# Layer 0's first convolution block: all late taps but the last as VectorE products with GpSimd sums, with moved far taps, another bank layout in layer 1 and a moved weight load

## The chip, the cores and the metric

One NeuronCore of a Trainium2 chip runs the whole kernel in one launch. The metric is the device time of one execution in microseconds (us). The engines are TensorE (PE in the profile, with its weight loads as PEld), VectorE (DVE), ScalarE (ACT), GpSimd (POOL) and SyncE (SP), which issues most of the loads and stores.

## The reference

Two encoder layers on 1024 tokens of width 1024, all in float32. Cut to what matters here:

```python
for l in range(DEPTH):
    h = _rmsnorm(x, g_mix[l])
    p = h @ w_in[l]
    q = (_rmsnorm(p[..., :o1], g_q[l]) @ w_uq[l])        # 8 heads, 64 + 32 rotary
    kv = (_rmsnorm(p[..., o1:o2], g_kv[l]) @ w_ukv[l])   # keys 64 and values 64 a head
    y_attn = _mla_attention(q_nope, q_rope, k_nope, k_rope, v)
    a, gt = jnp.split(p[..., o3:], 2, axis=-1)
    u = a * jax.nn.sigmoid(gt)                           # 512 channels
    u = _dwconv(u, w_dw_conv[l], b_dw_conv[l])           # 31 taps along the tokens
    u = jax.nn.silu(_layernorm(u, g_conv_ln[l], b_conv_ln[l]))
    x = x + jnp.concatenate([y_attn, u], axis=-1) @ w_o[l]
    z = _dwconv(_rmsnorm(x, g_ffn[l]) @ w_up[l], w_dw_ffn[l], b_dw_ffn[l])
    zg, zv = jnp.split(z, 2, axis=-1)
    x = x + (jax.nn.silu(zg) * zv) @ w_down[l]
return _rmsnorm(x, g_final)
```

The 31-tap depthwise convolution is what the change is about. Channels lie on the 128 partitions, so the 512 channels are four blocks (0 to 3) of 128 x 1024, and each tap is a shifted multiply and add of a whole block.

## The kernel before, in words

Every float32 matrix product is made of three products of split operands (an upper part `h` and a lower part `l`), with 512 columns a matmul. Each layer runs through three stages, each with its own set of the eight PSUM banks: `project` (all products with `w_in`, `w_uq` and `w_k`), `attention` (64 steps, one for each head and block of 128 queries), and `feed` (the output product `w_o`, then `w_up` and `w_down` with a sum scheme of seven products in place of eight). The order of instructions on each engine is the order in which the code is written; nothing reorders it.

The taps of the depthwise convolution are done in three ways, by the numbers of `NEAR_TAPS`, block for block:

- **Near taps** run in `project` on VectorE, one multiply-add each (`conv_step`). A small planner (`work`) writes them between the evictions of the projection, by a count of VectorE's time in `clock["dve"]`.
- **Far taps** run in `project` too (`tap_far`): ScalarE multiplies into a buffer of the tag `wr`, which has three, and GpSimd issues a DMA that adds the buffer to the block.
- **Late taps** are what is left, and run in `attention` (`tap_late`). By default GpSimd multiplies and issues a DMA that adds the product to the block (`kinds` "pool"). For the first taps of block 0 listed in `STEP_AT` for layer 0, VectorE makes the product at a given step and GpSimd adds it to the block with an instruction of its own one step later (kind "step"). In layer 1 all late taps go the first way.

All adds to one block depend on each other: a sum of GpSimd on block 0 waits until the last accumulating DMA on block 0 has landed, and a DMA that adds to a block waits for the one before it on the same block. GpSimd runs its list in order. On the same list stand `yt<-yt,rb` (the division of a pair of heads, line 1670), whose result ScalarE splits eight steps after the even head's turn (`ys_3h`, line 194), and from step 50 the four loads of `wo` (line 915), whose lower parts ScalarE begins at step 55 (line 175). ScalarE runs in order too; it also copies half of every transposed probability tile (`pt`, line 1610), and VectorE the other half (line 1611). TensorE needs both for the next transposes (`t`) and for the value product (`o`).

In `attention` PSUM holds two wide tiles of two banks (scores `s`, later also the spread reciprocals `rc_70s` and the early output sums `po_e`), two single banks (`pv`, `o`, later `rc_71s`) and two banks `t0`, `t1` for transposes. A stage hands out banks in the order in which its tags are first used, so `pv` of the first two row tiles, which use `t0` and `t1`, get the first two banks of the set. At the end of a head `gather` adds the two halves of `o`: a copy on ScalarE (line 1647) and an add on VectorE (line 1648). For the last head `divide` (line 1683) and `finish` (the split `ys_7h`, `ys_7l`) follow. `next_sections` begins layer 1: norms, then the first three products, with `supply` calling for the loads and the lower parts of later weights.

Of the kernel before, what the change touches and what calls it, by code (L numbers as in the profile page):

```python
# [9 lines left out]
F32 = mybir.dt.float32  # L10
# [56 lines left out]
MANUAL = [E.PE, E.DVE, E.Activation, E.Pool]  # L67
LATE_COST = {"pool": 2.3, "step": 0.0}
LATE_STEPS = 0
STEP_AT = ((8, 12, 16, 20, 30, 36, 46, 50), ())  # L70
LATE_FROM = 2
NEAR_TAPS = ((8, 16, 18, 16), (16, 17, 18, 16))
BEGIN = (-5.7, -20.2)
GLU_AT = (-1.7, -14.9)
KEY_AT = (4.0, -8.6)
# [44 lines left out]
class Encoder:  # L120
# [395 lines left out]
    def next_sections(self, l, nxt, supply):  # L516
        names = ("g0", "a0", "g1")
        w = [self.complete(*e) for e in nxt["w"]]
        for k in range(8):
            self.norm_apply(l, nxt["x"], nxt, 1, k)  # L520
        self.norm_sums(l, nxt["x"], nxt, 1, range(4, 8))
        supply(-16.0)
        self.pp.tile([128, T], F32, name=f"skip{l}", tag="w1", bufs=1)
        ps = [self.wide(f"p{n}{l}") for n in names]
        self.key_weight(l, nxt["wk"])
        self.upper_first(ps[0], self.tiled(w[0]), nxt["hl"], HALVES[0])
        for i, c in ((1, 0), (0, 1), (1, 1)):
            for k in range(8):
                self.partial(ps[i], self.tiled(w[i]), nxt["hl"], k, (c,))
                if (i, c, k) == (0, 1, 3):  # L530
                    self.norm_spread(l, nxt, 1, self.bank)
            if (i, c) == (1, 0):
                self.norm_root(l, nxt, 1, self.bank)
        keys = self.key_products(l, nxt["wk"], lambda k, c: nxt["x"][k][:, c])
        for c in range(2):
            for k in range(8):
                self.partial(ps[2], self.tiled(w[2]), nxt["hl"], k, (c,))
        return nxt["hl"], nxt["r"], dict(zip(names, ps)), lambda: keys
# [38 lines left out]
    def project(self, l, carry):  # L577
        nc, a = self.nc, self.a
        par = self.par[l]
        clock = {"pe": 0.0, "dve": 0.0}  # L580
# [29 lines left out]
        def launch(steps, n=-1):  # L610
            active.append([clock["pe"], steps, n])

        def finish(n):
            for e in [e for e in active if e[2] <= n]:
                for step in e[1]:
                    clock["dve"] = max(clock["dve"], e[0]) + step[0]
                    e[0] = clock["dve"] + step[1]
                active.remove(e)
# [13 lines left out]
        def glu(j):  # L632
# [6 lines left out]
            todo = [t for t in range(KC) if t != PAD]  # L639
            taps.extend((j, t) for t in todo[:NEAR_TAPS[l][j]])  # L640
            taps.sort(key=lambda e: NEAR_ORDER.index(e[0]))
            away[j] = todo[NEAR_TAPS[l][j]:]
            far_at[j] = 0.0
# [210 lines left out]
        times, starts, t = {}, {}, 0.0  # L854
# [6 lines left out]
        def supply(now, turn=TURN):  # L861
            while coming and coming[0][1] <= now + LEAD:
                name, at = coming.pop(0)
                turning.append((name, at, self.cast(l, name)))
            while turning and turning[0][1] <= now + turn:
                name, at, e = turning.pop(0)
                w[name] = self.complete(*e)
# [10 lines left out]
        for n, (name, weight, emit, evict, after) in enumerate(seq):  # L878
            supply(clock["pe"])
            finish(n - 3)  # L880
            ps[name] = self.wide(f"p{name}{l}")
            emit()
            clock["pe"] += times[name]
            queue = [i for i, _ in taps]
            far = [j for j in away if clock["pe"] >= far_at[j] and
                   (j not in queue or queue.count(j) == NEAR_TAPS[l][j] and queue.index(j) > 8)]
            for j in sorted(far, key=far_at.get)[:FAR_TOGETHER if times[name] > 5.0 else 0]:
                self.tap_far(l, j, away[j].pop(0), u[j], conv[j])
                far_at[j] = clock["pe"] + FAR_GAP
            work(clock["pe"])  # L890
            if after:
                after()
            launch(evict(), n)
# [27 lines left out]
    def feed(self, l, conv, ys, ready, casts, x):  # L921
        nc, a, par = self.nc, self.a, self.par[l]
        left, right = HALVES
        steps, at = [], defaultdict(list)

        def put(step, rank, f):
            at[step].append((rank, len(at[step]), f))

        self.wo_steps(l, conv, ys, ready, casts, x, steps, put)
        self.up_steps(l, steps, put)  # L930
        out = self.down_steps(l, steps, put)
        for n in range(min(at), len(steps)):
            if n >= 0:
                steps[n]()
            for _, _, f in sorted(at.pop(n, ()), key=lambda e: e[:2]):
                f()
        return out
# [619 lines left out]
    def attention(self, l, u, conv, away, spill, keys, kvs, loaded, ahead, wo, begun):  # L1557
# [2 lines left out]

        qd, qrd, kd = spill
        state, v = {}, []

        def rows(tt):
            (kv, wv), ts = kvs, slice(tt * 128, (tt + 1) * 128)
# [50 lines left out]
        def values(pair, n):  # L1616
            h, qp = divmod(pair, 4)
            st = state[h]
            e = h % 2
            gg = qp // 2  # L1620
            main, aux = slice(e * 64, e * 64 + 64), slice(64 - e * 64, 128 - e * 64)
            if qp % 2 == 0:
                if gg == 0 and e == 0:
                    st["y"], st["rb"] = self.blk(f"yt{l}_{h}"), self.blk(f"rb{l}_{h}")
                elif gg == 0:
                    st["y"], st["rb"] = state[h - 1]["y"], state[h - 1]["rb"]
                st["po"] = self.bank(f"o{l}_{h}_{gg}")
            po = st["po"]
            cs = slice(qp % 2 * 256, qp % 2 * 256 + 256)
            for g in range(2):  # L1630
                pt = st["pt"].pop((qp, g)).rearrange("p k q r t -> p k (q r t)")
                for i in range(4):
                    k = 4 * g + i
                    nc.tensor.matmul(po[ROW_TILES[i % 2], cs], v[k // 2][:, k % 2, h * 64:h * 64 + 64], pt[:, i, :],  # L1634
                                     start=k < 2, stop=k > 5)
            if qp % 2 == 0:
                return
            if n >= total:
                gather(h, gg, main, aux, n)
            else:  # L1640
                agenda[n].append(lambda: gather(h, gg, main, aux, n))

        def gather(h, gg, main, aux, n):
            st = state[h]
            y, rb, po = st["y"], st["rb"], st["po"]
            qs = HALVES[gg]
            nc.scalar.copy(out=y[main, qs], in_=po[aux, :])
            nc.vector.tensor_tensor(out=y[main, qs], in0=po[main, :], in1=y[main, qs], op=ALU.add)
            if h < HEADS - 2:
                if gg:  # L1650
                    agenda[n + 1].append(lambda: turned(h, main, rb, y))
            elif n > total:
                divide(y[main, qs], main, h, gg)
            else:
                agenda[n + 1].append(lambda: divide(y[main, qs], main, h, gg))
                if h == last:
                    agenda[n + 1].append(lambda: finish(last, y, 0))
# [24 lines left out]
        def divide(ym, main, h, c):  # L1682
            nc.vector.tensor_tensor(out=ym, in0=inv.pop((h, c))[main, :], in1=ym, op=ALU.mult)
# [10 lines left out]
        def finish(h, y, c):  # L1694
            cs = HALVES[c]
            if c == 0:
                ys.append([self.blk(f"ys{l}_{h}{i}", F32R) for i in "hl"])
            hi, lo = (t[:, cs] for t in ys[-1])
            nc.scalar.copy(out=hi, in_=y[:, cs])
            nc.vector.scalar_tensor_tensor(out=lo, in0=y[:, cs], scalar=1.0, in1=hi.bitcast(F32), op0=ALU.mult, op1=ALU.subtract)  # L1700
# [3 lines left out]
        agenda = defaultdict(list)  # L1704
        late = sorted(((i + 0.5) / len(away[j]), j, t) for j in range(4) for i, t in enumerate(away[j]))
        stepped = [i for i, (_, j, _) in enumerate(late) if j == LATE_STEPS][:len(STEP_AT[l])]
        kinds = ["step" if i in stepped else "pool" for i in range(len(late))]
        costs = [LATE_COST[kind] for kind in kinds]
        for i, (_, j, t) in enumerate(late):
            n = LATE_FROM + int((SIDE_TIME - LATE_FROM) * sum(costs[:i]) / sum(costs))  # L1710
            if kinds[i] == "step":
                m, tap = STEP_AT[l][stepped.index(i)], self.tap_late(l, j, t, u[j], conv[j], nc.vector)
                agenda[m].insert(0, lambda tap=tap: next(tap))
# [7 lines left out]
        last = HEADS - 1  # L1721
# [11 lines left out]
        for n in range(-2, total + 1):  # L1733
            if n % 2 and n > 2:
                values((n - 3) // 2, n)
# [8 lines left out]
            if n + 2 < total:  # L1744
                h, qt = divmod(n + 2, 8)
# [199 lines left out]
```

## Time and profile before

| what | value |
|---|---|
| median of 3 runs | 2239.71 us (2237.3 to 2240.65) |
| profiled execution, its own time | 2242.22 us |
| its span, first to last instruction | 2240.5 us |
| TensorE busy | 2221.1 us, 99% of the span, 12750 matmuls |
| VectorE busy | 1666.4 us, 74% |
| ScalarE busy | 1240.2 us, 55% |
| GpSimd busy | 681.7 us, 30% |
| mean granted TensorE clock | 0.997 |
| chain that ended last | 86% TensorE, 5% VectorE, 3% issue, 3% DMA |

Busy time is summed over the whole span. A share says nothing of a single stage. "Granted clock" is the part of TensorE's full 2.4 GHz that the chip gave it; 0.5 is its lower level of 1.2 GHz.

### The profile page before, as it was taken

What the parts mean: (1) busy time and instruction counts of PE and PEld (TensorE: products, weight loads), DVE (VectorE), ACT (ScalarE), POOL (GpSimd) and SP (SyncE); (2) the same over time, 40 slices, a digit from 0 to 9 for tenths busy, and PEclk for the clock granted to TensorE, in tenths of its full rate; (3) what the DMA queues carried; (4) which work ended last, traced back from release to release, by engine and by line L of the source; (5) the groups of instructions that cost most, each with busy time, mean ns of one, the idle gap of its engine ahead of it and who ended that gap; (6) DMA issues with size and microseconds to landing.
All of it is one profiled execution on the core that took longest, in us unless ns stands there. A gap on an engine that the chain in (4) does not pass through costs nothing.

```text
span 2240.5 us, 34453 instructions
## 1 busy us (share of the span) xinstructions
PE 2221.1 (99%) x12750; PEld 1780.0 (79%) x12750; DVE 1666.4 (74%) x2213; ACT 1240.2 (55%) x1896; POOL 681.7 (30%) x791
## 2 busy tenths in 40 slices
PE   9999999999999999999999999999999999999998
PEld 7887666788888888888878876668888888888887
DVE  7998777668877776776579877776787777768765
ACT  5454776446655555544533557774575555555444
POOL 1232666332333333001412224652323333320032
PEclk9999999999999999999999999999999999999999
DMA  5799997765899998935957999976578999988366
GB/s 184 169 201 280 215 188 172 204 173 122 219 278 305 273 296 207 338 101 138 214 145 156 214 268 209 212 182 180 149 173 221 299 291 284 289 209 298 96 130 167
DMA packets 197928, 473.29 MB, mean 211 GB/s; under 512 B 24224, under 2 KB 32128, under 8 KB 197760
## 3 DMA queue, kind: packets, MB, share of 16 engines
q0 software_dynamic: 98912, 221.08, 48.6%
q1 hardware_dynamic: 98272, 248.96, 33.5%
q8 instruction: 100, 1.64, 0.3%
q10 hardware_dynamic: 576, 1.05, 0.1%
q14 instruction: 68, 0.56, 0.1%
HBM read 305.35 MB, written 80.40 MB: 172 GB/s over the span
## 4 chain that ended last, share of the span: by engine, by line
PE 86%; DVE 5%; issue 3%; DMA 3%; POOL 1%; ACT 1%; SPq 0%; POOLq 0%; ACTq 0%; DVEq 0%
PE p L1141 34%; PE pd L1329 17%; PE po L952 7%; PE s L1585 5%; PE o L1634 4%; PE pa L212 3%; PE t L1608 3%; PE pg L212 2%; PE pg L574 2%; PE pq L212 1%; PE pn L212 1%; DVE conv L1784 1%; PE pkv L212 1%; PE pa L574 1%; DVE mx L1587 1%
## 5 line engine op out<-in xcount | busy, mean ns | idle before, releaser
L1141 PE MATMUL p<-b,w 128*128 128x512 f32 x3552 | 807.2, 389 | 0.4 <-ACT zv L1152 0.3
L1141 PEld LDWEIGHTS p<-b,w 128*128 128x128 f32 x3552 | 666.0, 188 | 141.0 <-DVE w L1523 1.2
L1329 PE MATMUL pd<-ab,wd 128*128 128x512 f32 (+1 forms) x1920 | 422.3, 381 | 0.0
L1329 PEld LDWEIGHTS pd<-ab,wd 128*128 128x128 f32 x1920 | 350.7, 188 | 69.5 <-DVE ab L1523 0.4
L176 POOL DMA_DIRECT2D w<-wu x96 | 84.4, 880 | 358.2 <-ACT w L175 318.0
L1587 DVE TENSOR_REDUCE mx<-s 128x1 f32<-128x1024 f32 x128 | 156.3, 1221 | 38.3 <-PE s L1585 32.9
L1595 ACT ACTIVATE p<-s,mx 128x1024 f32<-128x1024 f32 x128 | 142.9, 1117 | 58.7 <-DVE mx L1587 56.2
L1535 DVE SCALAR_TENSOR_TENSOR o<-zg,par,o 128x1023 f32<-128x1023 f32 x88 | 112.8, 1283 | 76.5 <-ACT o L1529 75.1
L1784 DVE SCALAR_TENSOR_TENSOR conv<-gate,par,conv 128x1023 f32<-128x1023 f32 (+14 forms) x125 | 159.1, 1275 | 4.5 <-ACT conv L636 1.5
L176 POOL DMA_DIRECT2D w<-in_w_up x116 | 100.6, 868 | 202.0 <-ACT w L175 178.5
L1611 DVE COPY pt<-t 128x512 f32<-128x512 f32 x128 | 87.9, 687 | 64.1 <-PE t L1608 62.3
L175 ACT ACTIVATE w<-w 128x512 fp32r<-128x512 f32 x212 | 133.6, 630 | 3.0
L1634 PE MATMUL o<-pt,v 128*64 128x256 f32 x1024 | 129.3, 390 | 5.2 <-DVE pt L1611 2.3
L1090 DVE TENSOR_TENSOR zg<-p,zg 128x512 f32<-128x512 f32 x88 | 60.6, 690 | 99.1 <-PE p L1141 92.3
L1521 ACT CAST ab<-ac 128x512 fp32r<-128x512 f32 x130 | 80.1, 617 | 94.7 <-DVE ac L1264 93.3
L915 POOL DMA_DIRECT2D wd<-in_w_down x44 | 33.0, 750 | 308.1 <-PE pd L1329 301.1
L1535 DVE SCALAR_TENSOR_TENSOR v<-zv,par,v 128x1023 f32<-128x1023 f32 x88 | 112.5, 1280 | 10.4 <-ACT v L1529 10.3
L1521 ACT CAST w<-wu 128x512 fp32r<-128x512 f32 x84 | 51.9, 620 | 122.6 <-DVE wu L1090 122.6
L1634 PEld LDWEIGHTS o<-pt,v 128*64 128x64 f32 x1024 | 68.2, 137 | 57.5 <-issue 20.2
L1108 ACT CAST w<-wu 128x512 fp32r<-128x512 f32 x96 | 59.0, 614 | 93.0 <-DVE wu L1090 89.4
L1608 PEld LDWEIGHTS t<-ident,p 64*128 64x128 f32 x2048 | 77.1, 139 | 40.0 <-issue 27.4
L1523 DVE TENSOR_TENSOR ab<-ac,ab 128x512 fp32r<-128x512 f32 x130 | 89.3, 689 | 24.8 <-ACT ab L1521 17.7
(2123 smaller groups left out, 4304.3 us busy)
## 6 DMA issues: line engine op xcount, KB each, us to landing
w<-in_w_up POOLq DMA_DIRECT2D x232, 256.0 KB, 7.5
wu<-in_w_up SPq DMA_DIRECT2D x88, 512.0 KB, 4.8
w<-wu POOLq DMA_DIRECT2D x96, 256.0 KB, 5.6
sd<-in_w_down SPq DMA_DIRECT2D x44, 512.0 KB, 9.2
ws<-sd SPq DMA_DIRECT2D x44, 512.0 KB, 7.5
wd<-in_w_down POOLq DMA_DIRECT2D x88, 256.0 KB, 5.5
act<-v SPq DMA_DIRECT2D x36, 512.0 KB, 6.1
ac<-act SPq DMA_DIRECT2D x72, 256.0 KB, 5.7
```

The costliest lines, as they stand in the source:

```text
L175: self.nc.scalar.activation(out=lo, in_=hi.bitcast(F32), func=AF.Copy, scale=-1.0)
L176: self.nc.gpsimd.dma_start(out=lo, in_=src, accum_op=ALU.add)
L212: nc.tensor.matmul(ps[:, HALVES[c]], w, x[:, HALVES[c]], start=(k == 0 and s == 0), stop=(k == n - 1 and s == 2))
L952: self.nc.tensor.matmul(ps, p[:, sl], q[:, cs], start=(k == 0 and t == 0), stop=(k == 3 and t == 2))
L1141: nc.tensor.matmul(ps, w[p][:, k * 128:(k + 1) * 128], b[:, q], start=(i in (1, 5, 2) and k == 0 and t == 0), stop=(k == 3 and t == 2), sk ...
L1329: nc.tensor.matmul(ps[t, m][:, cs], w[i, j][p][:, m * 128:(m + 1) * 128], b[:, q, cs], start=(i in (1, 5, 2) and j == 0 and s == 0), stop= ...
L1535: self.nc.vector.scalar_tensor_tensor(out=o[:, a:b], in0=z[:, at + a:at + b], scalar=self.par[l][:, tap:tap + 1], in1=o[:, a:b], op0=ALU.m ...
L1587: nc.vector.tensor_reduce(out=mx, in_=ps, op=ALU.max, axis=AX.X, negate=True)
L1595: nc.scalar.activation(out=p, in_=ps, func=AF.Exp, bias=mx, accum_out=st["sums"][:, qt:qt + 1])
L1608: nc.tensor.transpose(t[:, i, qi, :], st["p"][2 * qp + qi][r, ks], self.ident[r, r])
L1634: nc.tensor.matmul(po[ROW_TILES[i % 2], cs], v[k // 2][:, k % 2, h * 64:h * 64 + 64], pt[:, i, :], start=k < 2, stop=k > 5)
L1784: self.nc.vector.scalar_tensor_tensor(out=y[:, lo:hi], in0=u[:, lo + s:hi + s], scalar=self.tap(l, j, t), in1=y[:, lo:hi], op0=ALU.mult, o ...
```

## The change

Five edits:

1. Block 0 of layer 0 has 14 late taps. Before, 8 were VectorE products with GpSimd sums and 6 were GpSimd products with adding DMAs, mixed on one block. Now 13 are VectorE products with sums, at the steps listed, and the last tap alone is a GpSimd product with a DMA. Block 3 of layer 0 loses one near tap, which becomes a far one, and one that was far is now late; layer 1 gets three more near taps (two for block 0, one for block 2), and so three fewer late ones.
2. In `project`, VectorE work due in the first half of a section, and what ScalarE does with it, is written ahead of the far taps of that section.
3. In layer 1, `attention` uses its two wide tiles and its two single banks once before anything else, which gives them the first six banks, and `t0` and `t1` the last two; `feed` gets a matching order of its banks.
4. For the first half of the last head, `gather` is written one step later, in both layers, and what follows it too.
5. In `next_sections` the call `supply(-16.0)` stands behind the spread of the norm.

```diff
-STEP_AT = ((8, 12, 16, 20, 30, 36, 46, 50), ())
+STEP_AT = ((8, 10, 12, 14, 16, 18, 20, 30, 32, 34, 36, 46, 48), ())
-NEAR_TAPS = ((8, 16, 18, 16), (16, 17, 18, 16))
+NEAR_TAPS = ((8, 16, 18, 15), (18, 17, 19, 16))
...
-        supply(-16.0)
         self.pp.tile([128, T], F32, name=f"skip{l}", tag="w1", bufs=1)
...
                 if (i, c, k) == (0, 1, 3):
                     self.norm_spread(l, nxt, 1, self.bank)
+                    supply(-16.0)
...
+            work(clock["pe"] - times[name] / 2)
             for j in sorted(far, key=far_at.get)[:FAR_TOGETHER if times[name] > 5.0 else 0]:
                 self.tap_far(l, j, away[j].pop(0), u[j], conv[j])
...
         steps, at = [], defaultdict(list)
+        for i in (3, 2, 4, 5, 6, 7) if l else ():
+            self.pp.tile([128, 512], F32, name=f"lay{l}_{i}", tag=f"d{i}", bufs=1)
...
         state, v = {}, []
+        for i, f in enumerate((self.wide, self.wide, self.bank, self.bank) if l else ()):
+            f(f"lay{i}")
...
             if n >= total:
                 gather(h, gg, main, aux, n)
             else:
-                agenda[n].append(lambda: gather(h, gg, main, aux, n))
+                m = n + (h == last)
+                agenda[m].append(lambda: gather(h, gg, main, aux, m))
```

The first place is GpSimd's list in layer 0's attention, around the division of the second pair of heads (`late_0_27` is tap 27 of block 0, `conv_0` the block, `yt_2` the pair of heads). Before:

```order
L1796 TENSOR_SCALAR late_3_27_3357<-gate_3_821,par_63 128x1012
L1802 DMA conv_3_892<-late_3_27_3357 128x1012
L1796 TENSOR_SCALAR late_0_27_3399<-gate_0_417,par_63 128x1012
L1802 DMA conv_0_425<-late_0_27_3399 128x1012
L1800 TENSOR_TENSOR conv_0_425<-conv_0_425,late_0_22_3397 128x1017
L1796 TENSOR_SCALAR late_2_28_3504<-gate_2_665,par_63 128x1011
L1802 DMA conv_2_754<-late_2_28_3504 128x1011
L1670 TENSOR_TENSOR yt_2_2553<-yt_2_2553,rb_2_2554 128x1024
```

And now:

```order
L1802 TENSOR_SCALAR late_1_28_3404<-gate_1_420,par_63 128x1011
L1808 DMA conv_1_570<-late_1_28_3404 128x1011
L1806 TENSOR_TENSOR conv_0_425<-conv_0_425,late_0_27_3402 128x1012
L1802 TENSOR_SCALAR late_2_28_3509<-gate_2_662,par_63 128x1011
L1808 DMA conv_2_751<-late_2_28_3509 128x1011
L1676 TENSOR_TENSOR yt_2_2557<-yt_2_2557,rb_2_2558 128x1024
L1802 TENSOR_SCALAR late_3_27_3558<-gate_3_818,par_63 128x1012
L1808 DMA conv_3_886<-late_3_27_3558 128x1012
L1802 TENSOR_SCALAR late_3_28_3643<-gate_3_818,par_63 128x1011
L1808 DMA conv_3_886<-late_3_28_3643 128x1011
```

The sum ahead of `yt_2` no longer stands behind an adding DMA on the same block; taps 27 and 28 of block 3 now follow each other.

The second place is ScalarE in layer 0's projection, where the keys' and queries' latents are split (`far_0_16` is a far tap's product, `kvs`, `cqs` the split latents that TensorE needs next). Before:

```order
L175 ACTIVATE wu20l<-wu20h 128x768
L1790 ACTIVATE far_0_16_1221<-gate_0_417,par_63 128x1023
L1790 ACTIVATE far_1_21_1224<-gate_1_420,par_63 128x1018
L1790 ACTIVATE far_2_20_1227<-gate_2_665,par_63 128x1019
L664 ACTIVATE qss_1_1233<-cq_1231 128x1024
L720 ACTIVATE kvs_0h<-ckv_965,par_63 128x1024
L720 ACTIVATE kvs_1h<-ckv_1037,par_63 128x1024
L720 ACTIVATE cqs_1h<-cq_1231,par_63 128x1024
```

And now:

```order
L175 ACTIVATE wu20l<-wu20h 128x768
L664 ACTIVATE qss_1_1224<-cq_1222 128x1024
L720 ACTIVATE kvs_0h<-ckv_956,par_63 128x1024
L720 ACTIVATE kvs_1h<-ckv_1030,par_63 128x1024
L720 ACTIVATE cqs_1h<-cq_1222,par_63 128x1024
L1796 ACTIVATE far_0_16_1240<-gate_0_417,par_63 128x1023
L1796 ACTIVATE far_1_21_1243<-gate_1_420,par_63 128x1018
L1796 ACTIVATE far_2_20_1246<-gate_2_662,par_63 128x1019
```

The three far products moved behind the four splits.

The third place is VectorE at the end of layer 0's attention (the same rows stand in layer 1). Before:

```order
L1587 TENSOR_REDUCE mx_7_7_4573<-s_7_7_4562 128x1
L1648 TENSOR_TENSOR yt_6_4073<-o_7_0_4434,yt_6_4073 64x512
L1611 COPY pt_7_21_4600<-t_7_211_4583 128x8x64
L1676 RECIPROCAL rc_71_4611<-sums_7_4235 128x4
L1683 TENSOR_TENSOR yt_6_4073<-rc_70s,yt_6_4073 64x512
L1700 SCALAR_TENSOR_TENSOR ys_7l<-yt_6_4073,ys_7h 128x512
L1611 COPY pt_7_30_4645<-t_7_301_4628 128x8x64
L1810 TENSOR_TENSOR lns_0_4391<-lns_0_4391,lns_1_4431 128x1024
L1611 COPY pt_7_31_4684<-t_7_311_4667 128x8x64
```

And now:

```order
L1592 TENSOR_REDUCE mx_7_7_4575<-s_7_7_4564 128x1
L1616 COPY pt_7_21_4600<-t_7_211_4583 128x8x64
L1682 RECIPROCAL rc_71_4611<-sums_7_4237 128x4
L1654 TENSOR_TENSOR yt_6_4076<-o_7_0_4436,yt_6_4076 64x512
L1616 COPY pt_7_30_4642<-t_7_301_4625 128x8x64
L1816 TENSOR_TENSOR lns_0_4393<-lns_0_4393,lns_1_4433 128x1024
L1689 TENSOR_TENSOR yt_6_4076<-rc_70s,yt_6_4076 64x512
L1706 SCALAR_TENSOR_TENSOR ys_7l<-yt_6_4076,ys_7h 128x512
L1616 COPY pt_7_31_4686<-t_7_311_4669 128x8x64
```

The add `yt_6<-o_7_0` moved behind `pt_7_21` and the reciprocal, and the division and the split behind `pt_7_30` and the sum `lns`. On ScalarE the copy that `yt_6<-o_7_0` waits for moved in the same way, from ahead of its `pt_7_21` to behind the last exponential and the lower part of a `wo` weight. TensorE's list is the same row for row.

## Rows read from the trace of the kernel before

**Rows 1.** TensorE's waits: engine, line, releaser: us in total, times, longest.
```profile
PE o L1634 <- DVE pt L1611: 2.3, 7, 0.6
PE o L1634 <- ACT pt L1610: 1.9, 1, 1.9
PE t L1608 <- ACT pt L1610: 1.7, 1, 1.7
PE pv L1569 <- DVE qn L775: 1.3, 1, 1.3
...
PE pv L1569 <- DVE v L1573: 0.9, 1, 0.9
PE t L1608 <- DVE pt L1611: 0.5, 1, 0.5
PE pu L212 <- DVE kl L735: 0.5, 1, 0.5
```

**Rows 2.** Windows: equal work in layers 0 and 1, twice; the clock follows POOL.
```profile
327.86:342.26 14.40, 12.67 (x138) 8.44 (x137) 7.89 (x10) 9.23 (x16) 13.21 (x12) 0.88 0.84 173
1441.66:1452.54 10.88, 10.88 (x137) 7.71 (x136) 7.70 (x10) 9.29 (x16) 7.80 (x7) 1.00 0.79 161
366.69:381.96 15.27, 13.39 (x142) 8.89 (x141) 8.65 (x12) 7.91 (x15) 10.88 (x9) 0.89 1.05 259
1476.03:1487.64 11.61, 11.61 (x143) 8.06 (x141) 8.65 (x12) 8.19 (x15) 9.07 (x6) 1.00 0.59 157
```

**Rows 3.** ScalarE's timeline in those two stretches: start, duration, [idle before].
```profile
330.71 1.05 ACT L194 CAST ys_3h<-yt 128x1024 fp32r<-128x1024 f32 x1 [2.21 <-POOL yt L1670]
...
373.94 0.63 ACT L175 ACTIVATE wo<-wo 128x512 fp32r<-128x512 f32 x1 [3.83 <-DMA wo<-in_w_o]
```

**Rows 4.** GpSimd's timeline, layer 0's attention.
```profile
323.58 2.38 POOL L1800 TENSOR_TENSOR conv<-conv,late 128x1017 f32<-128x1017 f32 x1 [9.39 <-DVE ones L1660]
...
327.98 2.69 POOL L1670 TENSOR_TENSOR yt<-yt,rb 128x1024 f32<-128x1024 f32 x1
...
344.52 1.47 POOL L1796 TENSOR_SCALAR late<-gate,par 128x1010 f32<-128x1010 f32 x1
...
354.93 2.35 POOL L1800 TENSOR_TENSOR conv<-conv,late 128x1016 f32<-128x1016 f32 x1 [7.75 <-DVE yt L1648]
...
364.41 2.53 POOL L915 DMA_DIRECT2D wo<-in_w_o  x4
```

**Rows 5.** The chain that ended last, one piece: start, us, what.
```profile
346.28 8.50 DMA conv<-late
```

**Rows 6.** GpSimd's late taps, layer 0: duration ns min/median/max, and landings.
```profile
L1796 POOL TENSOR_SCALAR late<-gate,par x38: 1109/1442/1534, 206.5 to 368.9; 128x1014 f32<-128x1014 f32 x4, 128x1013 f32<-128x1013 f32 x4, 128x1012 f32<-128x1012 f32 x4, 128x1011 f32<-128x1011 f32 x4
L1802 POOL DMA_DIRECT2D conv<-late x38: 877/897/933, 207.9 to 370.7; - x38
L1800 POOL TENSOR_TENSOR conv<-conv,late x8: 2347/2377/2759, 234.1 to 366.6; 128x1022 f32<-128x1022 f32 x1, 128x1021 f32<-128x1021 f32 x1, 128x1020 f32<-128x1020 f32 x1, 128x1019 f32<-128x1019 f32 x1
...
DMA to landing us min/median/max: 4.6/8.4/12.8
```

**Rows 7.** VectorE's late products, layer 0: all eight, and one of them.
```profile
L1796 DVE TENSOR_SCALAR late<-gate,par x8: 745/754/1960, 233.3 to 356.7; 128x1022 f32<-128x1022 f32 x1, 128x1021 f32<-128x1021 f32 x1, 128x1020 f32<-128x1020 f32 x1, 128x1019 f32<-128x1019 f32 x1
...
344.57 1.96 DVE L1796 TENSOR_SCALAR late<-gate,par 128x1016 f32<-128x1016 f32 x1
```

**Rows 8.** VectorE's timeline, the end of layer 0's projection.
```profile
194.74 1.23 DVE L775 TENSOR_TENSOR qn<-pn,rq 128x1024 f32<-128x1024 f32 x1 [2.51 <-PE pn L212]
```

**Rows 9.** ScalarE's and TensorE's timelines, the last head of layer 0.
```profile
394.04 0.63 ACT L175 ACTIVATE wo<-wo 128x512 fp32r<-128x512 f32 x1
...
395.72 0.65 PE L301 MATMUL rc_71s<-ident,rc 128*128 128x128 f32 x4
```

**Rows 10.** VectorE's and TensorE's timelines, the end of layer 1's attention.
```profile
1511.02 1.29 DVE L1692 TENSOR_TENSOR y<-po_e,y 128x512 f32<-128x512 f32 x2
...
1511.26 0.39 PE L952 MATMUL po<-ys_1h,wo 128*128 128x512 f32 x1
```

## Prediction

> **What bounds the kernel now.** I first read the shares of busy time: TensorE 99%, every other engine below 75%. The chain that ended last is TensorE to 86%. So the time is TensorE's own work plus its waits, and time saved or added elsewhere counts only where TensorE waits for it. The second view is therefore the list of what TensorE waits for [rows 1]. The waits are few: two long ones, 1.9 and 1.7 us, both for ScalarE's half of the probability tiles, one of 1.3 and some of 0.5 to 0.9 us. Nothing else there can be taken away.
>
> A long wait costs more than itself, and this is the third view, windows over equal work [rows 2]. Layer 1 does the same steps without the stall, so it is the measure. The stretch with the 1.7 us wait takes 14.40 us against 10.88, that with the 1.9 us wait 15.27 against 11.61: 3.52 and 3.66 us. Of the first, 14.40 - 12.67 = 1.73 us is the wait, and 12.67 - 10.88 = 1.79 us is matmuls at the lower of the two clock levels, 1.2 GHz: the granted clock is 0.88 over the stretch, after TensorE had stood idle, against 1.00 in layer 1. The second is alike (1.88 and 1.78).
>
> Then I followed each stall back. ScalarE's timeline [rows 3] shows it standing 2.21 us before `ys_3h`, for GpSimd's `yt`, and 3.83 us before a lower part of `wo`, for the load; the `pt` copies are behind these. GpSimd's timeline [rows 4] shows why both are late. Its sum on block 0 stands idle 9.39 us at 323.58, and `yt` follows at 327.98. Another stands idle 7.75 us at 354.93, and the `wo` loads are issued only at 364.41. The releasers named beside the two sums are VectorE instructions that have nothing to do with them; the sum must wait for the last adding DMA on its block. The chain of waits shows it for the second: 8.50 us in DMA `conv<-late` from 346.28 [rows 5], and that DMA takes 4.6 to 12.8 us to land [rows 6].
>
> **The change, part by part. Edit 1, first stall.** Block 0 gets no adding DMA before its tap 30, so the 9.39 us go. GpSimd's list gets longer: five more sums of 2.38 us (11.9), one product with issue more (block 3), and five of block 0's fewer, at 1.44 + 0.90 = 2.34 us [rows 6]. Net 11.9 + 2.34 - 11.7 = 2.5 us, taken as if all lay ahead of `yt`. It begins at 327.98 - 9.39 + 2.5 = 321.1 and ends 2.69 later at 323.8; ScalarE wants it at 330.71 - 2.21 = 328.5 [rows 3, 4]. Margin 4.7 us. Gain **3.5**.
>
> **Edit 1, second stall.** The last sum now belongs to the product of step 48. The products of steps 8 and 50 span 233.3 to 356.7 [rows 7], so a step is about 2.9 us, and step 48 comes near 344.57 + 5.9 = 350.5. Product 0.75, sum 2.38, product and issue of tap 30 2.34: the loads are issued at 356.0. From issue to use took 373.94 - 364.41 = 9.5 us, so they land at 365.5. ScalarE wants them at 373.94 - 3.83 = 370.1. Margin 4.6 us. Gain **3.7**. On the way taps 27 and 28 of block 3 are adjacent on GpSimd, and the second DMA waits for the first to land: with a landing of 8.4 us less one product, GpSimd may stand some 6 us there. From the end of `yt_2` at 323.8 to the last product at 350.5 lie 26.7 us, with nine instructions or pairs of 2.3 to 2.7 us ahead of the last sum, about 21.4: slack 5.3 us. With the margin of 4.6 a stand of 6 us is just covered, with 3.9 left.
>
> **Edit 1, price on VectorE.** Five more products of 0.754 us, and each may hold up a `pt`. VectorE is not full, but one product of eight took 1.96 us, from 344.57, when a GpSimd product ran from 344.52 [rows 4, 7], and TensorE's 0.5 us wait for VectorE's `pt` belongs to such a delay [rows 1]. At the same rate thirteen have about two: one more such wait, **-0.5**. Bounds: +0.5 if none is hit; four hit, each paying its whole 1.96 - 0.75 = 1.2, gives -4.8.
>
> A rule speaks against this part. The Trainium skill (SBUF — State Buffer, Who interferes with whom) calls the port pair that VectorE and GpSimd share an exclusive lock: whichever starts first keeps it for its whole instruction. The 1.96 us row agrees in direction; by that rule a product that meets a sum would be held up to 2.38 us, and the sum would be that of the slower rival below.
>
> **Edits 1 and 2, the end of layer 0's projection.** One tap less on VectorE, and taps written earlier, into an idle time such as the 2.51 us before `qn` [rows 8]. So the copies of `v` come earlier, and TensorE's 0.9 us wait for them goes [rows 1]: **+0.9**, bounds 0 and 0.9. The far products move behind ScalarE's four splits; VectorE's `kl` needs the upper parts, and the 0.5 us wait of `pu` for it goes: **+0.5**, bounds 0 and 0.5. The later far taps have the rest of the projection as cover. Layer 1's three extra near taps run beside TensorE's projection, where VectorE waits for TensorE; I count nothing, and up to -1 if that cover is gone.
>
> **Edit 3.** In layer 1 the first `pv` waits 1.3 us for `qn` [rows 1], since it takes the bank that `qn` reads. Now `pv` gets other banks, and the bank `qn` reads goes to a wide tile used later. **+1.3**, bounds 0.5 and 1.3. In `feed` the new order lets an output product take the bank of an early sum that VectorE has yet to add. It begins at 1511.26; the first of VectorE's two adds ends at 1511.02 + 1.29 / 2 = 1511.67 [rows 10]. **-0.4**, bounds 0 and 1.05 (both adds).
>
> **Edit 4, both layers.** VectorE's `pt_7_21` no longer stands behind the add on `o_7_0`. But `rc_71s` takes the bank of `o_7_0`, so it now waits for that add. The copy ahead of it stands behind ScalarE's `wo` part, which ends at 394.04 + 0.63 = 394.67; copy and add have no row here, and I take 0.65 us each, as half of the pair of adds [rows 9, 10]: 395.97, against 395.72 when `rc_71s` ran. That is 0.25, called **-0.3** a layer, -0.6 in all. Bounds: a gain of 0.65 a layer if the earlier `pt` ends a wait, a loss of 0.9 a layer if one more instruction comes between.
>
> **Edit 5.** It moves ScalarE's lower parts behind the spread, where no wait of TensorE stands: nothing; up to -0.5 if a lower part then comes late.
>
> **The sum.** Gains 3.5 + 3.7 + 0.9 + 0.5 + 1.3 = 9.9; losses 0.5 + 0.4 + 0.6 = 1.5; net -8.4 us. The profiled execution took 2242.22 us, so 2233.8; the median of the runs is 2.5 lower, 2239.71, so **2231.3 us**, 0.38% faster.
>
> **The rivals.**
> *One stall stays.* GpSimd may wait elsewhere, at block 3's adjacent DMAs or in its own longer list. For it: a landing reaches 12.8 us [rows 6], and the margins of 4.7 and 4.6 us are smaller than the spread of landings. Against: no block-0 sum stands behind a DMA. Net -8.4 + 3.6 = -4.8: 2234.9, and 2237 with two more hit products.
> *The change only moves the waits.* Both stalls come back, because ScalarE's need is met by a GpSimd that is itself full. Then -8.4 + 7.2 = -1.2: 2238.5. Against: 17 us of idle time in two places go, and 2.5 us of work come.
> *Slower: VectorE's products are held by GpSimd's sums.* Place: steps 10 to 48, where sums now follow products closely. A product held for a whole sum takes 0.75 + 2.38 = 3.1 us, 2.4 too long; the `pt` behind it is as late as ScalarE's was when TensorE waited 1.7 to 1.9, and each such stall cost 3.6 with the lower clock behind it [rows 2]. Three (10.8) eat the gain of 8.4, four (14.4) end 6 us slower: 2245.7. For it: the 1.96 us product. Against: the median of the eight is 754 ns and the least 745 [rows 7], so meetings with sums were rare, and with five times as many sums as hits so far, four in thirteen is much.
>
> **How the numbers follow.** Main case 0.60; one stall stays 0.20; the waits move 0.11; slower 0.09. About 0.2%, 4.5 us, is what a measurement can tell from no change: below 2235.2 is faster, above 2244.2 slower. Main case: all faster. One stall: about two thirds faster (2234.9 lies close to the line). Waits move: same. So faster 0.73, same 0.18, slower 0.09. The best bounds (both pt gains, 0.5 and 1.3, in place of their losses) add 2.9: 2228.4, and a little of the 2.3 us in seven short waits for VectorE's `pt` [rows 1] makes 2227. Upwards the range takes in one stall with its price, 2237.5. What is left out is the moved waits and the slower case, 2 in 10.
>
> **What would show it.** In the profile after: the two windows at 10.9 and 11.6 us with clock 1.00; ScalarE not idle before `ys_3h` and the `wo` part; GpSimd's sums idle only for VectorE's products; `wo` issued near 356; no `pv<-qn`, `pv<-v` and `pu<-kl` among TensorE's waits; short new ones at `rc_71s` and `po`. Wrong would be: late products of 2 to 3 us on VectorE with a `pt` behind each, granted clock below 1.00 in new places, or GpSimd standing before block 3's tap 28 with `wo` late again.

## The result, and the profile after

The changed kernel takes 2250.21 us (median of 5 runs, 2249.61 to 2251.43) against 2239.09 before: 0.5% slower, ratio 1.005, 95% interval 1.0035 to 1.0065. The forecast was 2231.3, with 2237.5 as the upper end. The profiled execution took 2249.61 us with a span of 2247.8, so 7.3 us more than the span of before. By the medians the loss is 11.1 us; the profiled execution of before was itself 3.1 us above its median.

TensorE's waits of the changed kernel, with total, times and longest, answer to [rows 1]:

```profile
PE pu L212 <- DVE kl L735: 13.8, 2, 8.2
PE rc_71s L301 <- DVE yt L1654: 2.0, 2, 1.0
...
PE o L1639 <- DVE pt L1616: 1.1, 5, 0.2
PE t L1613 <- DVE pt L1616: 1.0, 3, 0.4
PE po L955 <- DVE y L1698: 0.3, 1, 0.3
```

Both long waits for ScalarE's `pt` are gone, and so are those of `pv` for `qn` and `v`. One wait that was 0.5 us is now 13.8 us: `pu`, the rotary queries' product in the projection, for `kl`, once in each layer (5.66 and 8.18 us). That is the wait of which I said that edit 2 would take it away.

Windows of the changed kernel (columns as in [rows 2]: start and end, length, then busy us and number of instructions of TensorE, its weight loads, VectorE, ScalarE and GpSimd, then granted clock, DMA share and GB/s). The first two are the stretch from the last keys' product through `pu` to the start of `pn` in layers 0 and 1, the last two are the attention stretches of [rows 2]:

```profile
164.55:184.07 19.52, 13.86 (x60) 11.08 (x58) 8.29 (x16) 5.61 (x7) 2.63 (x3) 0.83 1.06 316
1277.20:1299.73 22.53, 14.35 (x59) 11.43 (x58) 10.65 (x19) 5.61 (x7) 2.64 (x3) 0.77 1.06 291
332.86:343.75 10.89, 10.89 (x137) 7.72 (x136) 7.70 (x10) 9.28 (x16) 8.54 (x7) 1.00 0.76 155
367.69:379.31 11.62, 11.62 (x142) 8.05 (x140) 8.65 (x12) 8.20 (x15) 9.09 (x6) 1.00 0.77 196
```

The same work in the kernel before, for the first two:

```profile
165.47:178.22 12.75, 12.24 (x57) 9.79 (x57) 11.71 (x19) 3.93 (x5) 1.64 (x3) 1.00 1.01 287
1279.45:1291.35 11.90, 11.90 (x60) 9.92 (x58) 9.58 (x18) 4.00 (x6) 1.32 (x2) 1.00 1.03 272
```

The attention stretches came out as forecast: 14.40 to 10.89 and 15.27 to 11.62 us, 3.51 and 3.65 us gained at clock 1.00. The projection lost 19.52 - 12.75 = 6.77 us and 22.53 - 11.90 = 10.63 us, together 17.4, with the granted clock at 0.83 and 0.77. Of the 6.77 us, the wait is 5.66 (19.52 - 13.86) in place of 0.51, and 13.86 - 12.24 = 1.62 us is matmuls at the lower level of 1.2 GHz behind it; in layer 1 the two parts are 8.18 and 2.45 us. The sum 17.4 - 7.16 = 10.2 us less 2.9 us, spread over the other five stretches of the span, is the 7.3 us.

**Where the projection's wait comes from.** ScalarE's timeline of the changed kernel, layer 0 and layer 1, and two rows of layer 0's attention that answer to [rows 3]:

```profile
153.55 3.21 ACT L1796 ACTIVATE far<-gate,par 128x1023 f32<-128x1023 f32 x3
...
170.14 0.84 ACT L175 ACTIVATE wu10l<-wu10h 128x768 fp32r<-128x768 f32 x1 [9.56 <-DMA wu10h<-in_w_uq]
170.89 2.82 ACT L733 CAST kh<-pk 128x1024 fp32r<-128x1024 f32 x3
...
333.41 1.03 ACT L194 CAST ys_3h<-yt 128x1024 fp32r<-128x1024 f32 x1
...
370.80 0.64 ACT L175 ACTIVATE wo<-wo 128x512 fp32r<-128x512 f32 x1
...
1285.31 0.84 ACT L175 ACTIVATE wu11l<-wu11h 128x768 fp32r<-128x768 f32 x1 [9.74 <-DMA wu11h<-in_w_uq]
```

ScalarE no longer stands before `ys_3h` and the `wo` part. But it stands 9.56 and 9.74 us before the lower part of a weight of the projection, `wu10l` and `wu11l`, whose load has not landed. Behind it on ScalarE are the copies `kh`, the upper parts of the keys; VectorE's lower parts `kl` need `kh`, and `pu` needs the bank that `kl` reads. It is the same kind of stall as the one the change removed. GpSimd's timeline of the changed kernel shows why the load is late, and below it the two that answer to [rows 4]:

```profile
154.99 0.86 POOL L1797 DMA_DIRECT2D conv<-far  x1 [7.25 <-DMA conv<-far]
156.01 0.84 POOL L1797 DMA_DIRECT2D conv<-far  x1 [0.16 <-issue]
157.05 0.83 POOL L1797 DMA_DIRECT2D conv<-far  x1 [0.19 <-issue]
157.59 1.04 POOL L171 DMA_DIRECT2D wu10h<-in_w_uq  x1
...
324.26 2.72 POOL L1676 TENSOR_TENSOR yt<-yt,rb 128x1024 f32<-128x1024 f32 x1
...
358.29 2.49 POOL L916 DMA_DIRECT2D wo<-in_w_o  x4
...
1273.31 0.73 POOL L171 DMA_DIRECT2D wu11h<-in_w_uq  x1 [0.34 <-issue]
```

The same loads in the kernel before, GpSimd's timeline:

```profile
152.10 1.04 POOL L171 DMA_DIRECT2D wu10h<-in_w_uq  x1
...
1266.37 1.06 POOL L171 DMA_DIRECT2D wu11h<-in_w_uq  x1
```

A section's load stands behind its far taps on GpSimd's list. Edit 2 moved the far products behind four splits on ScalarE; GpSimd waits for them before it can issue the adding DMAs, and the load follows: 157.59 - 152.10 = 5.5 and 1273.31 - 1266.37 = 6.9 us later. The row at 154.99 names an earlier adding DMA as what ended GpSimd's idle time, but that one had landed by 150.81 (138.70 + 12.11, below); what GpSimd still lacked was the first of the three far products, which ScalarE began at 153.55 and which take some 1.1 us each. The chain of waits of the changed kernel passes through this load (start, us, what):

```profile
138.70 12.11 DMA conv<-far
...
157.59 12.53 DMA wu10h<-in_w_uq
```

Before, the load took 9.8 us from issue to landing, by the view of its tile:

```profile
DMA to landing us min/median/max: 9.8/9.8/9.8
```

So it lay ready at 161.9, and ScalarE began on it in this row of its timeline, without idle time ahead:

```profile
163.59 0.83 ACT L175 ACTIVATE wu10l<-wu10h 128x768 fp32r<-128x768 f32 x1
```

The margin was 1.7 us, and the load came 8.2 us later (5.5 in the issue, 2.7 in the transfer). In layer 1 the load took 10.5 us before and landed at 1276.9, 1.0 us ahead of its use at 1277.85; now it takes 12.0 us and comes 8.4 us later. Why the transfers take longer was not tested. The Trainium skill (Perfetto Trace Analysis, DMA Instruction — SWDGE (GPSIMD)) says that the issue's row ends when the descriptors are made and not when the data have moved; the rows agree, 1.04 us against 9.8 and 12.5.

### The profile page after: what moved, and what is told of

It reads as the page before. It is cut to its first block, busy times and chain, and to the rows that moved or that the text cites. A ratio compares the mean times of both kernels' runs of the same rounds, so it can differ in the third digit from the quotient of the medians.

```text
span 2247.8 us, 34428 instructions
## 1 busy us (share of the span) xinstructions
PE 2220.4 (99%) x12750; PEld 1781.9 (79%) x12750; DVE 1674.3 (74%) x2220; ACT 1242.0 (55%) x1896; POOL 677.4 (30%) x782
## 4 chain that ended last, share of the span: by engine, by line
PE 83%; DVE 6%; DMA 5%; issue 4%; ACT 1%; POOL 1%; POOLq 0%; ACTq 0%; SPq 0%; DVEq 0%
PE p L1144 33%; PE pd L1332 17%; PE po L955 7%; PE s L1590 6%; PE o L1639 5%; PE pa L212 3%; PE t L1613 3%; PE pg L212 2%; PE pg L574 2%; PE pn L212 1%; DMA conv<-far 1%; DVE conv L1790 1%; PE pv L1574 1%; PE pu L212 1%; PE pa L574 1%
## 5 line engine op out<-in xcount | busy, mean ns | idle before, releaser
L1538 DVE SCALAR_TENSOR_TENSOR v<-zv,par,v 128x1023 f32<-128x1023 f32 x88 | 112.5, 1281 | 10.5 <-ACT v L1532 10.4
```

Of the source, the lines that this page charges most:

```text
L1538: self.nc.vector.scalar_tensor_tensor(out=o[:, a:b], in0=z[:, at + a:at + b], scalar=self.par[l][:, tap:tap + 1], in1=o[:, a:b], op0=ALU.m ...
```

## The experiments

**Without edit 2, and edit 2 alone.** The edit of the first, and the opposite of it on the kernel before for the second:

```diff
-            work(clock["pe"] - times[name] / 2)
```

> The changed kernel without edit 2 alone: the one line that writes VectorE's work ahead of a section's far taps is left out. Theory: edit 2 holds GpSimd's list until ScalarE's far products are made, so a weight load behind them on the list is issued 5.5 us (layer 0) and 6.9 us (layer 1) later, ScalarE stands for it, and TensorE waits 5.7 and 8.2 us for kl and then runs part at the lower clock: 17 us in all. Without it TensorE waits at most 0.5 us for kl, and what is left is the gain of the other edits, some 9 us against before: about 2230 (0.996). Rival A: the numbers of taps (edit 1's near, far and late taps) fill ScalarE's and GpSimd's lists in the projection; then TensorE's wait for kl stays at 5 us or more and the time above 2245. Rival B: the far taps were only half the cause; 2235 to 2240.

> The kernel before with edit 2 alone. Theory: TensorE waits 5 to 9 us for kl in each layer, loss 15 to 18 us with the lower clock behind it: about 2256 (1.0075); the waits of attention stay as they were. Rival A (numbers of taps): 2239 to 2243, with waits for kl of 1 us or less.

Without edit 2: 2234.58 us against 2238.97, ratio 0.9981 (0.9972 to 0.9989), faster. Edit 2 alone: 2254.96, ratio 1.0074 (1.0061 to 1.0087), 16 us slower. TensorE's waits of the kernel without edit 2, and then with edit 2 alone:

```profile
PE pa L574 <- DMA wa01l<-in_w_in: 0.6, 1, 0.6
...
PE pu L212 <- DVE kl L735: 0.5, 1, 0.5
```

```profile
PE pu L212 <- DVE kl L735: 14.8, 2, 9.3
PE o L1635 <- ACT pt L1611: 3.1, 1, 3.1
```

The loss is edit 2's: it comes with that line and goes with it, with the numbers of taps of before or of after; rival A falls. But the gain of the rest is 4.4 us against the median and not 9. That asked for an answer of its own (below).

**The loads ahead of the far taps.** Edit 2 stays; a section's load is issued before its adding DMAs:

```diff
             work(clock["pe"] - times[name] / 2)
+            supply(clock["pe"], TURN - times[name])
```

> The changed kernel with edit 2 kept, but a section's weight load is issued by GpSimd ahead of the section's adding DMAs for far taps. Only the place of the upper parts' loads on GpSimd's list differs. Theory (the late issue of the load is the cause): wu10h and wu11h are issued some 5 to 8 us earlier, ScalarE doesn't stand for them, TensorE's wait for kl falls below 1 us: about 2230 (0.996), as without edit 2. Rival C (the order on ScalarE or VectorE itself makes kl late, or the transfers are slow because the far taps' transfers run with them): kl is still late by 3 us or more, above 2243.

2244.45, ratio 1.0024 (1.0014 to 1.0033). Neither theory had it right. TensorE's waits:

```profile
PE s L1591 <- DMA qr<-rc: 6.6, 2, 4.2
```

The wait for `kl` is gone, so the late load did cause it. A new one of 4.2 and 2.4 us stands in its place: the first scores wait for the rotary queries `qr`, which SyncE copies by DMA. SyncE's timeline (start, us for the issues of a row) with the loads first, and then in the kernel before:

```profile
159.92 6.20 SPq L128 DMA_DIRECT2D kn<-kh  x4
...
168.65 6.47 SPq L128 DMA_DIRECT2D kn<-kl  x4
...
181.49 8.20 SPq L128 DMA_DIRECT2D kr<-krd  x8
```

```profile
163.10 2.70 SPq L128 DMA_DIRECT2D kn<-kh  x4
...
166.49 4.57 SPq L128 DMA_DIRECT2D kn<-kl  x4
...
178.65 8.45 SPq L128 DMA_DIRECT2D kr<-krd  x8
```

The issues for the keys' copies take 6.20 and 6.47 us in place of 2.70 and 4.57, just while the three moved adding DMAs run (issued at 154.9 to 157.0 in this run), and the copies `kr` behind them on SyncE begin 2.8 us later. To tell whether these transfers are the reason, the same kernel was run with the last three of them in each layer cut to 64 columns:

```diff
+LAST_FAR = [(0, 0, 16), (0, 1, 21), (0, 2, 20), (1, 0, 26), (1, 1, 23), (1, 2, 22)]
...
-        self.nc.gpsimd.dma_start(out=y[:, lo:hi], in_=p[:, lo:hi], accum_op=ALU.add)
+        end = lo + 64 if (l, j, t) in LAST_FAR else hi
+        self.nc.gpsimd.dma_start(out=y[:, lo:end], in_=p[:, lo:end], accum_op=ALU.add)
```

> The kernel with the loads first, but the last section's three adding DMAs for far taps in each layer (taps 16, 21, 20 and 26, 23, 22 of blocks 0, 1, 2) add only 64 of some 1,010 columns, so that part of the convolution is left out; every issue and order stays. With the loads first, SyncE's issues of kn<-kh from 160 took 6.2 us in place of 2.6 and kr<-krd began 3 us later, and TensorE waited 4.2 and 2.4 us for qr. Theory: the moved far transfers hold up SyncE's key transfers; with small ones kn<-kh takes under 4 us, TensorE's wait for qr is under 1 us, and the time is 2234 to 2237 (like the kernel without edit 2). Rival: qr is late for another reason (its products on VectorE, the loads issued earlier); the wait for qr stays above 2 us in layer 0.

2233.35, ratio 0.9973 (0.9964 to 0.9982), with less work done. SyncE's row and TensorE's wait in it:

```profile
159.79 3.58 SPq L129 DMA_DIRECT2D kn<-kh  x4
```

```profile
PE s L1592 <- DMA qr<-rc: 1.4, 2, 1.2
```

The issues fall from 6.20 to 3.58 us and the wait from 6.6 to 1.4 us in all, not quite to the 1 us expected, and 11 us go. So edit 2 has a second price: its transfers run beside the keys'.

**Edit 2 in all sections but the last.**

```diff
-            work(clock["pe"] - times[name] / 2)
+            if name != "q2":
+                work(clock["pe"] - times[name] / 2)
```

> The changed kernel with edit 2 in every section but one: in the last section that has far taps (q2) VectorE's work is written behind them, as before. Theory: of edit 2 only that section costs, since the load behind its far taps (wu10h, wu11h) is the one with the smallest margin, 1.7 us before its use in the kernel before; TensorE's wait for kl falls to 0.5 us and the time to that of the kernel without edit 2, 2234 to 2236. Rival: earlier sections hold up GpSimd's list too and the next load is late; wait for kl above 2 us in a layer, above 2238.

2248.61, ratio 1.0046 (1.0032 to 1.0059): the theory fell, the rival was right in its time, though not in its wait. TensorE's waits, and ScalarE's timeline in layer 0:

```profile
PE pk L212 <- ACT kvs_0h L720: 7.4, 2, 4.9
```

```profile
148.38 1.15 ACT L1797 ACTIVATE far<-gate,par 128x1023 f32<-128x1023 f32 x1 [2.21 <-DMA conv<-far]
150.86 1.15 ACT L1797 ACTIVATE far<-gate,par 128x1018 f32<-128x1018 f32 x1 [1.33 <-DMA conv<-far]
154.90 1.15 ACT L1797 ACTIVATE far<-gate,par 128x1019 f32<-128x1019 f32 x1 [2.89 <-DMA conv<-far]
```

Far products use three buffers, and each is free only when its adding DMA has landed. The earlier groups, moved later, now hold them when the last group begins; ScalarE stands 2.21 + 1.33 + 2.89 = 6.4 us, ahead of the split `kvs_0h`. So it is not one section alone: in both forms tried, the later far taps met another use with a small margin.

**Why the rest is worth 4.4 us and not 9.** The thirteen steps alone on the kernel before, and the kernel before profiled a second time:

```diff
-STEP_AT = ((8, 12, 16, 20, 30, 36, 46, 50), ())
+STEP_AT = ((8, 10, 12, 14, 16, 18, 20, 30, 32, 34, 36, 46, 48), ())
```

> The kernel before with the thirteen steps of STEP_AT alone: block 0's late taps of layer 0 as VectorE products with GpSimd sums, nothing else changed. Theory: ScalarE no longer stands before ys_3h and the wo part, the two stalls of attention go (3.5 and 3.7 us in the profiled execution of before), TensorE waits 0.3 to 1 us more for VectorE's pt: -5 to -7 us, about 2233 (0.997). Rival E: the two stalls of before are not there in every execution, since they hang on when a transfer lands; then the gain against the median of before is smaller, -2 to -4, 2235 to 2237, though the trace shows both stalls gone.

> The kernel before once more, for a second profile. If the two stalls of attention and the lower clock behind them are a fixed part of the kernel, both show again, with clock 0.88 and 0.89 in the two stretches and TensorE's waits of 1.7 and 1.9 us. Rival E: one or both are shorter or gone in this execution, and the time is lower by 3 to 5 us.

The steps alone: 2234.41 against 2238.7, ratio 0.9983 (0.9974 to 0.9992), with neither stall in the trace; 4.3 us, nearly the whole gain of the kernel without edit 2. The execution of the second profile of before took 2239.06 us. Its waits of TensorE, then GpSimd's sum and ScalarE's `ys_3h` in it:

```profile
PE o L1634 <- ACT pt L1610: 2.8, 1, 2.8
...
PE t L1608 <- ACT pt L1610: 0.4, 1, 0.4
```

```profile
322.19 2.34 POOL L1800 TENSOR_TENSOR conv<-conv,late 128x1017 f32<-128x1017 f32 x1 [8.65 <-DVE pt L1611]
```

```profile
329.28 1.05 ACT L194 CAST ys_3h<-yt 128x1024 fp32r<-128x1024 f32 x1 [0.86 <-POOL yt L1670]
```

The adding DMA ended 1.4 us earlier (the sum starts at 322.19, not 323.58), ScalarE stood 0.86 us and not 2.21, TensorE 0.4 and not 1.7, and the clock of this stretch stayed at 1.00. The two attention stretches of [rows 2] in this execution:

```profile
327.78:339.26 11.48, 11.10 (x138) 7.64 (x137) 7.79 (x10) 9.22 (x16) 10.59 (x9) 1.00 0.85 184
362.74:378.82 16.08, 13.24 (x142) 8.77 (x140) 8.65 (x12) 7.90 (x15) 13.05 (x13) 0.89 1.08 260
```

So the first stall, 3.5 us in the execution that I read, costs 11.48 - 10.88 = 0.6 us here: rival E. The second is there again and costs more, 16.08 - 11.61 = 4.5 us against 3.7. Two other runs have layer 0's attention as before, edit 2 alone and edit 3 alone (below): there the first stretch takes 10.88 and 10.89 us, without a stall, and the second 16.53 and 16.42. In these three executions the two stalls together cost 4.8 to 5.1 us, against 7.2 in the profile that the prediction read. Less the 0.5 us that `t` waits longer for VectorE's `pt`, that is the 4.3 us of the steps alone.

**The other edits.** Edit 3 alone on the kernel before (its two pieces as in the diff of the change), then the changed kernel without edits 2 and 4, without 2, 4 and 5, and without 2, 4, 5 and the extra near taps of layer 1. The piece for edit 4, and that for the near taps:

```diff
-                m = n + (h == last)
+                m = n
...
-NEAR_TAPS = ((8, 16, 18, 15), (18, 17, 19, 16))
+NEAR_TAPS = ((8, 16, 18, 15), (16, 17, 18, 16))
```

> The kernel before with edit 3 alone (the bank layouts of layer 1's attention and feed). Theory: TensorE's 1.3 us wait of pv for qn goes and one of 0.3 us of po for VectorE's y comes: -1.0 us, about 2238 (0.9996), too small to tell from no change by the times, so the trace decides. Rival: the wait only moves to the next use of the same bank; no change in the list of waits but its place.

> The changed kernel without edit 2 and without edit 4 (the first half of the last head's gather is not written a step later). Theory: edit 4 makes rc_71s wait 1.0 us for the add on o_7_0 in each layer and gives 0.3 to 0.7 back at pt_7_21, so leaving it out gains 0.6 to 1.4 us in all against the kernel without edit 2 alone: about 2229. Rival D: the earlier pt_7_21 is worth as much as the wait, within 0.4 us of the other, or slower than it.

> The changed kernel without edits 2, 4 and 5 (layer 1's extra near taps kept). Edit 5 was counted at nothing, but TensorE waits 0.6 us for the load of wa01l in one profile with it. Theory: edit 5 is worth nothing or costs up to 0.6 us: 2233 to 2234, the same as the kernel without edits 2 and 4 (2233.7) within 0.7 us. Rival: edit 5 is worth 1 us or more; above 2235.

> The changed kernel without edits 2, 4 and 5 and without layer 1's three extra near taps: what is left is the thirteen steps, block 3's near tap in layer 0, and the bank layouts. Theory: the new waits of layer 1 in the kernel without edit 2 (0.8 us of pk for kvs_1l, 0.6 us for the load of wa01l) come from the extra near taps and from the later lower part, which were counted at nothing, so this is 1 to 2 us faster than the kernel without edits 2 and 4: about 2232 (0.997). Rival: those edits cost nothing; within 0.5 us of the kernel without edits 2 and 4 (2233.7).

Edit 3 alone: 2241.08 against 2238.7, ratio 1.0012 (1.0003 to 1.0021), a little slower, where 1 us faster was expected. TensorE's waits in it (the first lies in layer 0, which this edit leaves as it was):

```profile
PE o L1638 <- ACT pt L1614: 3.2, 1, 3.2
...
PE s L1589 <- issue: 2.0, 1, 2.0
```

The wait of `pv` for `qn` is gone and one of 2.0 us has come, at 1358.8 in layer 1, ahead of `s<-kr,qr`. It is 1.0 us in the kernel without the extra near taps (2234.2) and not above 0.2 in that with them and without edit 2. So the near taps, which take adding DMAs out of layer 1's attention, seem to pay for edit 3's earlier start; that their transfers are the reason is argued, not shown.

Without edits 2 and 4: 2233.68, ratio 0.9976 (0.9966 to 0.9985), the best so far; edit 4 costs 0.9 us by the medians, within the 0.6 to 1.4 expected, though the two intervals overlap. Without edit 5 too: 2233.55, the same. Without the near taps as well: 2234.2, so they do not cost the 1 to 2 us expected.

## Why the prediction was wrong

**The step that failed.** "The far products move behind ScalarE's four splits; [...] **+0.5**, bounds 0 and 0.5. The later far taps have the rest of the projection as cover." I costed the move on ScalarE alone. What hangs on a far product is an adding DMA on GpSimd, behind it a weight load, behind that ScalarE's own lower part and `kh`. Measured, the term is -17.4 us by the windows, -16 us alone, and 15.6 us come back when it is left out of the changed kernel. The bounds left out the loss altogether, though [rows 3] showed the same pattern at `wo`: a load behind GpSimd's waits. The cover that I named at no price had a margin of 1.7 us in layer 0 and 1.0 in layer 1.

**Edit 1's stalls.** Right in the mechanism, and in the profiled execution in size: 3.51 and 3.65 us for 3.5 and 3.7. GpSimd's `yt` began at 324.26, with the projection's loss of some 5 us ahead of it, so at 319 in the time of the prediction, which said 321; the `wo` loads at 358.29, which less 5.0 us of loss and plus the 3.5 us of the first stall is 356.8, where it said 356. ScalarE used both without a stand, so the margins were there. GpSimd did stand before the second of block 3's adjacent DMAs, 4.16 us where up to 6 were put, and nothing on TensorE waited for it:

```profile
334.59 0.89 POOL L1808 DMA_DIRECT2D conv<-late  x1 [4.16 <-DMA conv<-late]
```

Wrong was to carry both stalls from one execution to the median: I took off the same 2.5 us, although the first stall was itself part of what made that execution longer. Three other executions of the same attention have 0 to 0.6 us for the first and 4.5 to 4.9 for the second; against the median the two gave 4.3 us.

**VectorE's products.** Thirteen of them, by duration (ns) least, median, longest:

```profile
L1802 DVE TENSOR_SCALAR late<-gate,par x13: 740/750/2341, 237.9 to 351.0; 128x1022 f32<-128x1022 f32 x1, 128x1021 f32<-128x1021 f32 x1, 128x1020 f32<-128x1020 f32 x1, 128x1019 f32<-128x1019 f32 x1
```

Three took 2.08 to 2.34 us, where I had counted two like the one of 1.96 us in the kernel before. One of them, and the GpSimd product beside it:

```profile
316.86 2.34 DVE L1802 TENSOR_SCALAR late<-gate,par 128x1012 f32<-128x1012 f32 x1
...
317.21 1.45 POOL L1802 TENSOR_SCALAR late<-gate,par 128x1011 f32<-128x1011 f32 x1
```

Each of the three ends 0.54 to 0.56 us after such a GpSimd product of 1.4 us, as the 1.96 us one of [rows 4, 7] does (0.54). TensorE's wait of `t` for VectorE's `pt` rose from 0.5 to 1.0 us, the -0.5 of the sum. The slower rival did not come: none was held for a whole sum, to 3.1 us. But none of the thirteen lies over a sum in this trace, so what such a meeting costs was not seen. By the rule of the Trainium skill (SBUF — State Buffer, Who interferes with whom) whichever of the two issues first has the shared ports for its whole instruction, and the other waits. The trace agrees that VectorE's product is held to the end of GpSimd's; it does not show the order, since by the rows the three held products began 0.12 to 0.35 us ahead of GpSimd's.

**The small terms.** The waits of `pv` in both layers went, as said. `rc_71s` waits 1.0 us in each layer, where 0.25 later was forecast; against that `o` no longer waits 0.63 us there (`pt` for `o`: 2.3 to 1.1 us in all). The net, -0.4 a layer, is the -0.3 of the sum. `po` waits 0.3 us (-0.4). Edit 5 is worth nothing, as said. Edit 3's +1.3 showed only together with the extra near taps of layer 1, which I had at nothing; that these are the reason is argued, as said above.

**The rivals.** None of them was the one that came. I looked for new waits where the change says that it acts, in attention, and gave the slower side 0.09, with attention as its place too. The projection, where one line moved the rows of three engines, had no rival.

## What to carry to other kernels

When an operation moves later on one engine, follow what it issues to the next queue and read the margin of everything behind it there, loads above all: issue, landing, first use. A load that was ready 1.7 us before its use was not covered here. A stall that hangs on when a transfer lands can be worth less or more than one profile shows (0 to 3.5 and 3.7 to 4.9 us here); profile more than once before it is put in a sum.

## What the runs showed of the hardware

SyncE's four issues for `kn<-kh` took 2.70 us, and 6.20 us while three adding DMAs of GpSimd moved some 500 KB each; with those cut to 64 columns 3.58 us. And the lower clock level stood behind the waits again: the windows with waits of 5.66 and 8.18 us were granted 0.83 and 0.77. But a wait of 1.95 us (`s` in layer 1, edit 3 alone) did not lower the clock of its stretch, while 1.73 us did in [rows 2]; what tells these two apart stays open:

```profile
1353.00:1366.00 13.00, 11.05 (x136) 7.62 (x134) 7.92 (x9) 9.70 (x15) 6.22 (x6) 1.00 1.02 210
```
